# Another order of the mixers' steps: a merge between the two halves of the retention, and a merge ahead of the LRU in the second layer

## The chip, the core and the metric

The kernel is one program on one core of a Trainium2 chip. The metric is the device time of one execution in microseconds (us): the median of three runs before the change is 2495.68 us. The engines of the core run side by side, each through its own fixed list of instructions: PE is TensorE (matrix multiplications), DVE is VectorE, ACT is ScalarE, POOL is GpSimd, SP is SyncE, which here only issues transfers from memory (DMA). An instruction starts when it is at the head of its engine's list and its semaphores are there. So the order in which the lists were written decides who stands behind whom.

## What is computed

Two layers, each a half feed-forward block, a mixer and a second half feed-forward block, on 256 tokens of a sequence ("latent", attending) and 256 tokens of context, 1024 channels. The second layer needs the context only as keys, values and states, so its later work is on 256 columns and that of the first layer on 512. The mixer has four branches (a gated linear recurrence, called LRU, windowed attention GQA, latent attention MLA, and retention), which are merged with gates:

```python
def _gated_merge(branches, gates, w_branch, w_out):
    br = jnp.stack(branches, axis=2)                       # 4 branches of 512 channels
    g = jax.nn.sigmoid(gates.reshape(B, T, N_BRANCH, D_MODEL))
    proj = jnp.einsum('btkw,kwd->btkd', br, w_branch)
    return jnp.einsum('btkd,btkd->btd', g, proj) @ w_out

def _rglru_coeffs(x, w_a, b_a, w_x, b_x, lam):             # LRU, per direction
    r = sigmoid(blockdiag(x, w_a) + b_a)
    i = sigmoid(blockdiag(x, w_x) + b_x)
    log_a = -LRU_C * r * softplus(-lam)
    return exp(log_a), sqrt(1 - exp(2 * log_a)) * (i * x)  # then h = a*h + b over time

# retention, per head, ends with a normalisation of its output:
yn = (y - mean(y)) * rsqrt(var(y) + LN_EPS)                # then * gn_g * silu(dg)
```

The sum over branches k doesn't depend on the order in which they are added, and a branch can be merged as soon as it is there.

## The kernel before

All matrices stand with channels on the 128 partitions and tokens in the columns. A weight tile comes by DMA (`load_w`, L175, three raw buffers), ACT rounds it to fp32r (L178, "hi"), DVE takes the rest (L179, "lo"), and PE runs three fp32r matmuls for each product (`mm3`, L191 to L193). So each weight tile of 128x1024 costs DVE one L179. There are four PSUM buffers "acc", two "s" (`pss`) and two "t" (`pst`).

The mixer runs its steps in the order of a table, `ORDER[l]` (L119 to L122), by `getattr(self, step)(*arg)` (L697), and then `finish` (the output projection and the normalisation). The steps: `gqa_in`, `gqa 0/1`; `mla_in`, `mla 0/1`; `lru_in` (projection and convolution), `lru`, `lru_out` (the gate of the LRU's output); `ret 0/1` (two heads of retention each); `merge k` (branch 0 is the LRU's, 1 GQA, 2 MLA, 3 retention). A scheduler places the instructions of later steps among those of earlier ones where the earlier have to wait, with the earlier step first whenever both are ready. So the table sets priorities, and not strict stages.

Three steps matter for what follows.

`merge k` (L1190) splits its branch (ACT L248, DVE L249, tiles `bh` and `bl`), and then for four pairs of output blocks runs the gates' product (`proj "gt"`), the branch's product, tanh on ACT (L1206), and the gating on DVE (L1212 in the first merge of a mixer, L1215 in others, with an addition on POOL). It is nearly pure PE work: 288 matmuls in the second layer, all on 256 columns. What it needs first from its branch are the tiles of head pair 0, and last those of the last head pair.

`lru` (L744) goes through two halves of four tiles. In each half: gate matmuls L768, tanh, exp, tanh on ACT (L769, L771, L772), DVE L773 to L775; then one sqrt over 128x2048 (L777), which needs another table of functions on ACT than tanh does, so a table load stands before it and one behind it; then matmuls L784, tanh L785, DVE L786 to L788 and two scans L793 and L795 for each tile, POOL L789 and L799. Two buffers `lu` are shared by all of it. In the second layer both halves use the same part of the array `Rall` for L769's result (L758), so the second half's L769 has to wait for the first half's scans and L799.

`ret hp` ends, for each of its two heads, with a chain: scores L1160, weights on DVE L1162, product L1168, two matmuls for mean and square L1175 and L1176, then DVE L1179, L1181, the ten instructions of `rsqrt` (L255 to L265), L1183 and L1185. Only then is the head's branch tile there, which `merge 3` splits.

In the first layer a queue of 24 steps for the modulation vectors (each four DVE instructions L408 on a 512 KB row block `mraw`, which takes one of the three raw buffers) is paced over the mixer's weight loads from the first merge on. The second layer's mixer has none.

Of the kernel before, what the change touches and what calls it, by code (L numbers as in the profile page):

```python
# [54 lines left out]
def host_constants():  # L55
# [40 lines left out]
    for kt in range(2):  # L96
# [20 lines left out]
P = {("g", 0): 20, ("g", 1): 16, "q": 18}  # L117

ORDER = [[("gqa_in",), ("gqa", 0), ("lru_in",), ("gqa", 1), ("mla_in",), ("lru",), ("lru_out",), ("merge", 1),  # L119
          ("mla", 0), ("merge", 0), ("mla", 1), ("ret", 0), ("ret", 1), ("merge", 2), ("merge", 3)],  # L120
         [("gqa_in",), ("gqa", 0), ("gqa", 1), ("mla_in",), ("lru_in",), ("lru",), ("merge", 1), ("mla", 0),
          ("lru_out",), ("mla", 1), ("ret", 0), ("ret", 1), ("merge", 0), ("merge", 2), ("merge", 3)]]  # L122


class Kernel:
# [1186 lines left out]
```

## Time and profile before

| | us |
|---|---|
| median of three runs (2492.79 to 2497.03) | 2495.68 |
| the profiled execution | 2495.55 |
| its span, first to last instruction | 2493.7 |
| PE busy in the span | 2421.7 |
| DVE busy | 1606.7 |
| ACT busy | 1053.7 |
| POOL busy | 389.1 |

The profiled execution is 0.13 us under the median, and 1.85 us of it lie outside the span. The mean granted clock of TensorE is 0.988 of its full 2.4 GHz. In the chain of work that ended last, PE holds 85% of the span, DVE 7%, ACT 3%, DMA 2%.

In rows of instructions the columns are: start (us from the span's start), duration (us), engine, line, operation, out<-in, tile on PE, shape, xcount (neighbours folded into one row), and in brackets the idle time before it and what ended that. An fp32 matmul of 512 columns leaves two records, an fp32r one leaves one. Rows of groups have busy us, mean ns of one, and idle time before with its releasers.

### The profile page before, as it was taken

The page shows a single profiled execution, that of the slowest core. Times are in us where ns is not written, and L with a number is a line of the kernel's source. Part 1 is how long each engine was busy: PE and PEld are TensorE (multiplying, and loading weights), DVE is VectorE, ACT ScalarE, POOL GpSimd, SP SyncE. Part 2 cuts the span into 40 slices and gives each one's busy share as a digit, 9 for nine tenths or more (in the row PEclk, how much of TensorE's full clock was granted, in tenths as well). Part 3 has the DMA queues.
Part 4 walks back from the last instruction along what each step waited for, and adds up shares of the span by engine and source line. Part 5 has one row for each costly group of instructions (what it writes and reads, how often), then busy time and mean ns, then how long its engine had stood idle before and what let it go on. Part 6 is the DMA issues. An engine that isn't in the chain of part 4 may idle for free.

```text
span 2493.7 us, 34785 instructions
## 1 busy us (share of the span) xinstructions
PE 2421.7 (97%) x13320; PEld 2043.8 (82%) x13320; DVE 1606.7 (64%) x2923; ACT 1053.7 (42%) x1694; POOL 389.1 (16%) x411
## 2 busy tenths in 40 slices
PE   7999999999999999999999999999999899999997
PEld 5888888776787778898888898888887678998997
DVE  4963338879857776469833379732388976766554
ACT  4322226665534323352222252322266764455443
POOL 2000024004011112340000220000240112223002
PEclk9999999999999999999999999999999999999999
DMA  8743234122433234437532357833341242465653
GB/s 308 236 136 101 93 108 152 37 89 76 142 88 111 82 97 145 139 120 254 185 93 93 107 174 259 286 100 95 99 145 60 86 128 78 135 194 160 185 177 114
DMA packets 289943, 340.71 MB, mean 137 GB/s; under 512 B 13505, under 2 KB 262625, under 8 KB 289777
## 3 DMA queue, kind: packets, MB, share of 16 engines
q1 hardware_dynamic: 285520, 323.88, 41.3%
q0 software_dynamic: 4256, 14.63, 1.7%
q8 instruction: 104, 1.70, 0.3%
q14 instruction: 63, 0.51, 0.1%
HBM read 334.26 MB, written 4.20 MB: 136 GB/s over the span
## 4 chain that ended last, share of the span: by engine, by line
PE 85%; DVE 7%; ACT 3%; DMA 2%; issue 2%; POOL 1%; SPq 0%; POOLq 0%; DVEq 0%; ACTq 0%
PE ffn01.acc L193 5%; PE ffn01.acc L191 5%; PE ffn01.acc L192 5%; PE ffn00.acc L191 5%; PE ffn00.acc L193 5%; PE ffn00.acc L192 5%; PE ffn10.acc L193 4%; PE ffn10.acc L191 4%; PE ffn10.acc L192 4%; PE ffn11.acc L191 3%; PE ffn11.acc L192 3%; PE ffn11.acc L193 3%; PE merge3.acc L192 1%; PE merge3.acc L191 1%; PE merge3.acc L193 1%
## 5 line engine op out<-in xcount | busy, mean ns | idle before, releaser
L179 DVE TENSOR_TENSOR ffn00.lo<-ffn00.raw,ffn00.hi 128x1024 fp32r<-128x1024 f32 (+1 forms) x71 | 86.5, 1220 | 135.2 <-ACT ffn00.hi L178 135.0
L179 DVE TENSOR_TENSOR ffn01.lo<-ffn01.raw,ffn01.hi 128x1024 fp32r<-128x1024 f32 (+1 forms) x71 | 87.8, 1237 | 128.2 <-ACT ffn01.hi L178 128.1
L179 DVE TENSOR_TENSOR ffn10.lo<-ffn10.raw,ffn10.hi 128x1024 fp32r<-128x1024 f32 (+1 forms) x71 | 87.1, 1226 | 124.9 <-ACT ffn10.hi L178 124.8
L178 ACT CAST ffn10.hi<-ffn10.raw 128x1024 fp32r<-128x1024 f32 (+1 forms) x71 | 72.8, 1025 | 186.5 <-PE ffn10.acc L192 101.9
L178 ACT CAST ffn01.hi<-ffn01.raw 128x1024 fp32r<-128x1024 f32 (+1 forms) x71 | 72.8, 1025 | 178.8 <-PE ffn01.acc L192 144.0
L178 ACT CAST ffn00.hi<-ffn00.raw 128x1024 fp32r<-128x1024 f32 (+1 forms) x71 | 72.5, 1025 | 174.5 <-PE ffn00.acc L192 136.9
L193 PE MATMUL ffn10.acc<-xh,ffn10.lo 128*128 128x512 f32 (+1 forms) x384 | 141.5, 372 | 0.6 <-DVE ffn10.lo L179 0.6
L192 PE MATMUL ffn01.acc<-xl,ffn01.hi 128*128 128x512 f32 (+1 forms) x384 | 142.0, 374 | 0.0
L193 PE MATMUL ffn01.acc<-xh,ffn01.lo 128*128 128x512 f32 (+1 forms) x384 | 141.7, 373 | 0.0
L192 PE MATMUL ffn10.acc<-xl,ffn10.hi 128*128 128x512 f32 (+1 forms) x384 | 141.4, 372 | 0.0
L191 PE MATMUL ffn10.acc<-xh,ffn10.hi 128*128 128x512 f32 (+1 forms) x384 | 140.9, 373 | 0.0
L191 PE MATMUL ffn01.acc<-xh,ffn01.hi 128*128 128x512 f32 (+1 forms) x384 | 140.7, 374 | 0.0
L191 PE MATMUL ffn00.acc<-xh,ffn00.hi 128*128 128x512 f32 x336 | 132.3, 395 | 2.7 <-ACT ffn00.hi L178 2.7
L193 PE MATMUL ffn00.acc<-xh,ffn00.lo 128*128 128x512 f32 x336 | 131.2, 392 | 0.0
L192 PE MATMUL ffn00.acc<-xl,ffn00.hi 128*128 128x512 f32 x336 | 131.1, 391 | 0.0
L179 DVE TENSOR_TENSOR ffn11.lo<-ffn11.raw,ffn11.hi 128x1024 fp32r<-128x1024 f32 x68 | 82.6, 1214 | 75.0 <-ACT ffn11.hi L178 75.0
L191 PE MATMUL ffn11.acc<-xh,ffn11.hi 128*128 128x256 f32 x352 | 99.6, 287 | 4.8 <-ACT xh L248 4.8
L192 PE MATMUL ffn11.acc<-xl,ffn11.hi 128*128 128x256 f32 x352 | 100.1, 286 | 0.0
L193 PE MATMUL ffn11.acc<-xh,ffn11.lo 128*128 128x256 f32 x352 | 99.8, 285 | 0.0
L178 ACT CAST ffn11.hi<-ffn11.raw 128x1024 fp32r<-128x1024 f32 x68 | 69.4, 1021 | 70.2 <-PE ffn11.acc L192 55.6
L193 PEld LDWEIGHTS ffn10.acc<-xh,ffn10.lo 128*128 128x128 f32 x384 | 72.0, 188 | 13.6 <-DVE ffn10.lo L179 1.0
L192 PEld LDWEIGHTS ffn01.acc<-xl,ffn01.hi 128*128 128x128 f32 x384 | 72.6, 190 | 12.7
(679 smaller groups left out, 7783.2 us busy)
## 6 DMA issues: line engine op xcount, KB each, us to landing
ffn10.mraw<-in_w_modT SPq DMA_DIRECT2D x48, 512.0 KB, 5.0
ffn00.raw<-in_ffn_w_in SPq DMA_DIRECT2D x44, 512.0 KB, 4.4
ffn01.raw<-in_ffn_w_in SPq DMA_DIRECT2D x44, 512.0 KB, 3.8
ffn10.raw<-in_ffn_w_in SPq DMA_DIRECT2D x44, 512.0 KB, 4.7
ffn11.raw<-in_ffn_w_in SPq DMA_DIRECT2D x44, 512.0 KB, 3.6
ret.raw<-in_w_in SPq DMA_DIRECT2D x32, 512.0 KB, 3.6
ffn01.mraw<-in_w_modT SPq DMA_DIRECT2D x32, 512.0 KB, 4.5
ffn00.mraw<-in_w_modT SPq DMA_DIRECT2D x24, 512.0 KB, 4.6
```

The lines of the kernel that those rows point to most:

```text
L178: nc.scalar.copy(out=hi[:, :n], in_=raw[:, :n])
L179: nc.vector.tensor_tensor(out=lo[:, :n], in0=raw[:, :n], in1=hi[:, :n].bitcast(F32), op=ALU.subtract)
L191: mm(out, wh, xh, start=start, stop=False)
L192: mm(out, wh, xl, start=False, stop=False)
L193: mm(out, wl, xh, start=False, stop=stop)
```

## The change

Only the table of steps changes.

```diff
-          ("mla", 0), ("merge", 0), ("mla", 1), ("ret", 0), ("ret", 1), ("merge", 2), ("merge", 3)],
-         [("gqa_in",), ("gqa", 0), ("gqa", 1), ("mla_in",), ("lru_in",), ("lru",), ("merge", 1), ("mla", 0),
-          ("lru_out",), ("mla", 1), ("ret", 0), ("ret", 1), ("merge", 0), ("merge", 2), ("merge", 3)]]
+          ("mla", 0), ("merge", 0), ("mla", 1), ("ret", 0), ("merge", 2), ("ret", 1), ("merge", 3)],
+         [("gqa_in",), ("gqa", 0), ("mla_in",), ("gqa", 1), ("lru_in",), ("merge", 1), ("lru",), ("mla", 0),
+          ("lru_out",), ("merge", 0), ("mla", 1), ("ret", 0), ("merge", 2), ("ret", 1), ("merge", 3)]]
```

In the first layer `merge 2` goes between `ret 0` and `ret 1`. In the second layer `mla_in` goes ahead of `gqa 1`, `merge 1` ahead of `lru`, `merge 0` ahead of `mla 1`, and `merge 2` between the two halves of the retention. Every engine has the same number of instructions as before.

On PE, in the second layer, at the LRU's first gate matmuls (L768; `lru_in.g` is the LRU's input, `lru.gw` its gate weights), the list was before:

```order
L192 MATMUL lru_in.acc_15879<-xl_92,lru_in.hi_15912 128x512
L193 MATMUL lru_in.acc_15879<-xh_84,lru_in.lo_15913 128x512
L768 MATMUL lru.pst_15956<-lru_in.g_15868,lru.gw_15950 128x512
L768 MATMUL lru.pst_15966<-lru_in.g_15868,lru.gw_15950 128x512
L191 MATMUL merge1.acc_16136<-xh_77,merge1.hi_16140 128x256
L192 MATMUL merge1.acc_16136<-xl_85,merge1.hi_16140 128x256
L193 MATMUL merge1.acc_16136<-xh_77,merge1.lo_16141 128x256
```

and after the change it is:

```order
L191 MATMUL merge1.acc_16333<-merge1.bh_15953,merge1.hi_16336 128x256
L192 MATMUL merge1.acc_16333<-merge1.bl_15957,merge1.hi_16336 128x256
L193 MATMUL merge1.acc_16333<-merge1.bh_15953,merge1.lo_16337 128x256
L768 MATMUL lru.pst_16372<-lru_in.g_15868,lru.gw_16366 128x512
L768 MATMUL lru.pst_16382<-lru_in.g_15868,lru.gw_16366 128x512
L768 MATMUL lru.pst_16392<-lru_in.g_15873,lru.gw_16366 128x512
L191 MATMUL mla.acc_16542<-mla_in.g_15579,mla.hi_16538 128x512
L192 MATMUL mla.acc_16542<-mla_in.g_15580,mla.hi_16538 128x512
L768 MATMUL lru.pst_16402<-lru_in.g_15873,lru.gw_16366 128x512
```

All 288 matmuls of `merge 1` stood behind the first L768 and now stand ahead of it. Between the first L768 and the first scores of `mla 0` (L882) there were 288 matmuls of `merge 1`, 63 of `mla 0` (12 of them on 512 columns), 23 of `lru_out` and the LRU's 16; now there are 63 of `mla 0`, 45 of `lru_out` and the 16.

On DVE, at the same place, the list was before:

```order
L179 TENSOR_TENSOR merge1.lo_16371<-merge1.raw_16368,merge1.hi_16370 128x1024
L773 TENSOR_SCALAR lru.g_16057<-lru.lu_16058 128x512
L773 TENSOR_SCALAR lru.g_16067<-lru.lu_16068 128x512
L774 SCALAR_TENSOR_TENSOR lru.lu_16058<-R,lru.g_16057 128x512
L179 TENSOR_TENSOR merge1.lo_16407<-merge1.raw_16404,merge1.hi_16406 128x1024
L775 SCALAR_TENSOR_TENSOR lru.g_16057<-lru.lu_16058,lru.g_16057 128x512
L774 SCALAR_TENSOR_TENSOR lru.lu_16068<-R,lru.g_16067 128x512
L179 TENSOR_TENSOR merge1.lo_16441<-merge1.raw_16438,merge1.hi_16440 128x1024
```

and after the change the same part of the LRU (second half, third and fourth tile) reads:

```order
L773 TENSOR_SCALAR lru.g_16473<-lru.lu_16474 128x512
L774 SCALAR_TENSOR_TENSOR lru.lu_16474<-R,lru.g_16473 128x512
L775 SCALAR_TENSOR_TENSOR lru.g_16473<-lru.lu_16474,lru.g_16473 128x512
L773 TENSOR_SCALAR lru.g_16483<-lru.lu_16484 128x512
L1046 COPY mla.g_16549<-mla_in.g_15529 32x512
L774 SCALAR_TENSOR_TENSOR lru.lu_16484<-R,lru.g_16483 128x512
L786 SCALAR_TENSOR_TENSOR lru.lu_16494<-lru.lu_16494,lru_in.g_15940 128x512
L775 SCALAR_TENSOR_TENSOR lru.g_16483<-lru.lu_16484,lru.g_16483 128x512
```

The subtractions and gatings of `merge 1` have left the LRU's part of the list; the copies of `mla 0` that its scores need (L1046, L1058, L1080, L1081) stand among or behind the LRU's last instructions.

On DVE, in the first layer, at the first head of `ret 0` (the list of weights L1147 and the first products L1162), the list was before:

```order
L179 TENSOR_TENSOR ret.lo_7230<-ret.raw_7227,ret.hi_7229 128x1024
L1136 SCALAR_TENSOR_TENSOR ret.g_6995<-ret.tmp_6993,ret.acc_6931 128x512
L179 TENSOR_TENSOR ret.lo_7270<-ret.raw_7267,ret.hi_7269 128x1024
L1136 SCALAR_TENSOR_TENSOR ret.g_6999<-ret.tmp_6997,ret.acc_6932 128x512
L1147 SCALAR_TENSOR_TENSOR ret.g_7001<-mla.g_6629,ffn00.lg_583,ret.tmp_7003 128x512
L1162 SCALAR_TENSOR_TENSOR ret.SW_7012<-ret.pss_7013,ret.g_7001 128x256
```

and after the change it is:

```order
L1136 SCALAR_TENSOR_TENSOR ret.g_6995<-ret.tmp_6993,ret.acc_6931 128x512
L408 SCALAR_TENSOR_TENSOR merge2.ht_7339,merge1.part_5008<-merge2.mraw_7337,merge2.sb_7183 128x512
L408 SCALAR_TENSOR_TENSOR merge2.ht_7341,merge1.part_5008<-merge2.mraw_7337,merge2.sb_7183 128x512
L179 TENSOR_TENSOR merge2.lo_7280<-merge2.raw_7277,merge2.hi_7279 128x1024
L1136 SCALAR_TENSOR_TENSOR ret.g_6999<-ret.tmp_6997,ret.acc_6932 128x512
L1147 SCALAR_TENSOR_TENSOR ret.g_7001<-mla.g_6629,ffn00.lg_583,ret.tmp_7003 128x512
L408 SCALAR_TENSOR_TENSOR merge2.ht_7343,merge1.part_5008<-merge2.mraw_7337,merge2.sb_7183 128x512
L408 SCALAR_TENSOR_TENSOR merge2.ht_7345,merge1.part_5008<-merge2.mraw_7337,merge2.sb_7183 128x512
L1162 SCALAR_TENSOR_TENSOR ret.SW_7012<-ret.pss_7013,ret.g_7001 128x256
```

Steps of the modulation queue that came with `merge 2` behind `ret 1` now stand ahead of the first L1162 of `ret 0`; their first L408 waits for a DMA of `mraw`.

## Rows read from the trace of the kernel before

**Rows 1.** The page's head and its first section, the whole span.
```profile
span 2493.7 us, 34785 instructions
PE 2421.7 (97%) x13320; PEld 2043.8 (82%) x13320; DVE 1606.7 (64%) x2923; ACT 1053.7 (42%) x1694; POOL 389.1 (16%) x411
```

**Rows 2.** Stretches: length, busy us by engine (records), granted clock, DMA share, GB/s.
```profile
816.00:862.00 46.00, 44.25 (x186) 34.00 (x186) 32.21 (x61) 15.47 (x24) 6.61 (x6) 1.00 0.24 70
878.00:930.00 52.00, 47.53 (x189) 36.54 (x188) 38.68 (x72) 15.30 (x24) 7.80 (x5) 0.93 0.28 84
894.30:901.00 6.70, 6.69 (x19) 5.44 (x20) 4.29 (x13) 0.37 (x1) 0.00 (x0) 0.60 0.25 77
1865.00:1930.00 65.00, 64.88 (x337) 47.19 (x336) 54.91 (x148) 40.35 (x91) 1.85 (x3) 1.00 0.20 62
1930.00:2011.00 81.00, 69.75 (x407) 56.49 (x407) 74.56 (x116) 54.45 (x75) 13.92 (x15) 0.92 0.32 96
...
2184.00:2253.00 69.00, 69.00 (x577) 69.00 (x576) 42.78 (x54) 34.64 (x52) 17.20 (x22) 1.00 0.64 195
```

**Rows 3.** PE's instructions in order of time, 1929 to 2017, second layer's LRU.
```profile
1930.04 1.88 PE L768 MATMUL lru.pst<-lru_in.g,lru.gw 128*128 128x512 f32 x4
...
1958.18 5.39 PE L768 MATMUL lru.pst<-lru_in.g,lru.gw 128*128 128x512 f32 x8 [2.79 <-ACT lru.lu L785]
...
2011.01 1.96 PE L882 MATMUL mla.pss<-mla.g,mla.q 96*128 96x512 f32 x4 [0.26 <-DVE mla.q L1080]
```

**Rows 4.** PE's groups of instructions, 1930 to 2011.
```profile
L768 PE MATMUL lru.pst<-lru_in.g,lru.gw 128*128 128x512 f32 x16 | 9.5, 718 | 2.8 <-ACT lru.lu L785 2.8
...
L193 PE MATMUL mla.acc<-mla_in.g,mla.lo 128*128 128x512 f32 x4 | 2.2, 600 | 1.3 <-DVE mla.lo L179 1.3
```

**Rows 5.** DVE's groups of instructions, 1930 to 2011.
```profile
L179 DVE TENSOR_TENSOR merge1.lo<-merge1.raw,merge1.hi 128x1024 fp32r<-128x1024 f32 x11 | 14.3, 1312 | 0.0
L788 DVE TENSOR_TENSOR lru.lu<-lru.lu,R 128x512 f32<-128x512 f32 x8 | 7.9, 1003 | 0.3 <-ACT R L777 0.3
...
L1212 DVE SCALAR_TENSOR_TENSOR R<-merge1.sa,merge1.acc 128x256 f32<-128x256 f32 x8 | 3.3, 412 | 1.5 <-PE merge1.acc L193 0.9 <-issue 0.5
L773 DVE TENSOR_SCALAR lru.g<-lru.lu 128x512 f32<-128x512 f32 x8 | 3.2, 416 | 0.0
```

**Rows 6.** ACT's groups of instructions, 1930 to 2011.
```profile
L771 ACT ACTIVATE lru.lu<-R,ffn00.c 128x512 f32<-128x512 f32 x8 | 6.3, 810 | 4.0 <-DVE R L795 2.8 <-DVE lru.g L775 1.2
...
L785 ACT ACTIVATE lru.lu<-lru.pst,ffn00.hb 128x512 f32<-128x512 f32 x8 | 5.3, 687 | 4.1 <-DVE R L795 4.1
L769 ACT ACTIVATE R<-lru.pst,ffn00.hb 128x512 f32<-128x512 f32 x8 | 5.2, 679 | 2.3 <-PE lru.pst L768 2.3
```

**Rows 7.** ACT in order of time, 1929 to 1960, around the first half's sqrt.
```profile
1945.74 1.28 ACT L777 ACT_TABLE_LOAD   x1
1947.04 1.92 ACT L777 ACTIVATE R<-R 128x2048 f32<-128x2048 f32 x1
1948.97 1.28 ACT L785 ACT_TABLE_LOAD   x1
```

**Rows 8.** PE in order of time, last head of the second layer's `ret 1`.
```profile
2158.41 0.61 PE L1176 MATMUL ret.pss<-ret.tmp,ffn10.onesh 128*128 128x256 f32 x2
```

**Rows 9.** DVE in order of time, the same head's chain, first and last instruction.
```profile
2160.05 0.41 DVE L1179 TENSOR_TENSOR ret.q<-ret.q,ret.pss 128x256 f32<-128x256 f32 x1
...
2167.87 0.64 DVE L1185 TENSOR_TENSOR ret.q<-ret.q,ret.q 128x256 f32<-128x256 f32 x1
```

**Rows 10.** PE in order of time, 886 to 905, first layer's `ret 1`, first head.
```profile
894.31 2.08 PE L1160 MATMUL ret.pss<-ret.g,ret.g 128*128 128x256 f32 x4 [3.87 <-DVE ret.SW L1162]
```

**Rows 11.** DVE in order of time, 880 to 940: that head's wait, then the second head's chain.
```profile
886.52 0.69 DVE L408 SCALAR_TENSOR_TENSOR merge2.ht<-merge2.mraw,ret.sb 128x512 bf16<-128x512 f32 x1 [3.87 <-DMA merge2.mraw<-in_w_modT]
...
922.46 0.69 DVE L1179 TENSOR_TENSOR ret.g<-ret.g,ret.pss 128x512 f32<-128x512 f32 x1 [2.48 <-ACT ret.tmp L1178]
...
935.49 0.69 DVE L1185 TENSOR_TENSOR ret.g<-ret.g,ret.g 128x512 f32<-128x512 f32 x1
```

## Prediction

> **What bounds the kernel now.** The page's first section comes first: PE is busy for 2421.7 of 2493.7 us [rows 1], so the time is PE's work plus the stretches in which PE waits. The change keeps every instruction, so it can only move those waits. Next I read the busy times by stretch. The merges of the second layer run without a gap: 577 matmuls of 256 columns in 69.00 us, 0.1196 us each [rows 2]. The waits that the change can reach are in three places. One is the LRU of the second layer (1930 to 2011): PE busy 69.75 of 81.00 us at a granted clock of 0.92, DVE busy 74.56 [rows 2]. The others are the retention's ends in the first layer: `ret 0` at 816 to 862, 1.75 us idle, and `ret 1` at 878 to 930, 4.47 us idle at a clock of 0.93 [rows 2]. The stretch of `gqa 1` and `mla_in` ahead of the LRU has PE at 64.88 of 65.00 us [rows 2], so there is nothing to gain there; exchanging these two is costed at nothing, and its cover is `lru_in` and `merge 1`, which are ready there.
>
> **The LRU of the second layer, before.** From the first L768 at 1930.04 to the first score of `mla 0` at 2011.01 [rows 3] there are 81.0 us. PE's work in them by count: the window has 407 records, of which 32 are the LRU's 16 fp32 matmuls (16 records of L768, and as many of L784), 12 are on 512 columns (three groups of four) [rows 4], and 363 on 256 (one stray one of 512 among them). At 0.1196 us these 363 are 43.4 us; the 12 at twice that are 2.9; four records of L768 took 1.88 us [rows 3], 0.9 us for a matmul without the last one's run-out, so 14.4 for 16. That makes 60.7 us of work and a **loss of 20.3 us**. DVE set the pace: it was busy 92% of the stretch, and in that, beside the LRU, it did 11 subtractions of `merge 1` (14.3 us) and its 8 gatings L1212 (3.3 us) [rows 5].
>
> **The same, after.** All 288 matmuls of `merge 1` now stand ahead of the first L768, where `gqa 1` and `lru_in` cover them. Behind it, up to the first score, PE's list holds 96 matmuls of 256 columns (11.5 us), the 12 (2.9) and the LRU's 16 (14.4): 28.8 us. How long the stretch becomes is DVE's and ACT's matter, since the scores need L1080 and L1081, which stand behind the LRU on DVE. From above: 81.0 less the 17.6 us of `merge 1` on DVE is 63.4. From below: the LRU's own work on DVE is eight groups of eight instructions, from L788 with 7.9 us to L773 with 3.2 [rows 5], 44.0 in all, and some 5 us of copies, rope and one or two subtractions stand in it, 49. To that come waits which `merge 1` filled on DVE before: each half's sqrt takes 1.28 + 1.92 + 1.28 us with its two table loads [rows 7], 4.5, under which DVE has one L775 (0.7) left, so 7.6 for both halves; the first load, L769 and L771 before DVE can begin (1.28 + 0.68 + 0.81, by [rows 6, 7]), 2.8; and the second half's L769, which waits for scans and POOL of the first, with ACT's waits for L795 of 2.8 and 4.1 us [rows 6] as the nearest rows, 3. That is 62.4. I take **62 us**, since both ways come out there. The loss becomes 62 - 28.8 = 33.2, **12.9 us more**. Bounds: 57 us (bare work and the sqrts alone), +7.9; 67 us (63.4, and eight of the LRU's matmuls on the chain at the 1.35 us of four in 5.39 [rows 3]), +17.9.
>
> The row shows what a table load does to ACT: it starts at 1945.74, takes 1.28 us, and the sqrt starts at 1947.04, with no further gap [rows 7]. The Trainium skill says otherwise ("ScalarE: Activation LUTs", section "What ACT_TABLE_LOAD costs"): a switch of tables costs the 1.28 us and a drain of about 1.38 us. By that the four loads inside the LRU would add an estimated 5.5 us to the chain; by the trace they add none, and I go by the trace.
>
> **Leaving the LRU.** After 3.87 us of idle PE [rows 10] the granted clock was 0.60 for the next 6.70 us [rows 2], half speed for most of it: 2.7 us lost. `mla 0` now starts after far more idle time. I add **2.5 us** (0 to 4).
>
> **merge 3 at the end of the second layer.** Before, `merge 0` and `merge 2` stood between `ret 1` and `merge 3`; now `merge 3` follows at once, and needs the last head's tile. From L1176 at 2158.41 [rows 8] to L1179 at 2160.05, then to L1185 at 2167.87 [rows 9]: 7.8 us, of which 0.7 was two L1215 that are gone from there, so 7.1; with 1.0 ahead, 0.6 for L1185 and 0.4 for the split, 9.1 us behind L1176. PE's list has 39 matmuls there, 4.7 us. PE waits 4.4; I take **4 us** (2 to 6).
>
> **merge 3 in the first layer.** The same, with 512 columns: L1179 at 922.46 to L1185 at 935.49 [rows 11] is 13.0 us, and with 0.9 ahead, 0.7 for L1185 and 0.7 for the split, 15.3. PE's list has 56 matmuls at 0.24, 13.4. **2 us** (0 to 4).
>
> **ret 0 in the first layer.** Its DVE list now has the modulation steps and weights of `merge 2` ahead of the first L1162, as `ret 1` had before. There an L408 waited 3.87 us for its `mraw` [rows 11], the head's weights came late, and PE idled 3.87 us [rows 10] and then ran at a clock of 0.60 [rows 2]. `ret 1` lost 4.47 + 2.7 = 7.2 us, `ret 0` 1.75; copying the pattern costs 5.4. It may be that the transfer is in time here, which costs nothing; I take **4** (0 to 5.4), nearer to the row. `ret 1` keeps its own pattern, as `merge 3` brings the modulation steps that `merge 2` brought, so nothing is won back. `merge 0` and `merge 2` of the second layer, as near-pure PE work, cost nothing where they now stand.
>
> **The sum**, against the profiled execution's 2495.55 us: 12.9 + 2.5 + 4 + 2 + 4 = 25.4, 2521 us; that execution lies 0.13 under the median, which changes nothing.
>
> **Rivals.**
> - *The LRU at its bare pace, and the tails filled (faster).* Free of `merge 1`, DVE goes through the LRU in 49 us, where the waits for sqrt are covered by the other tiles; then the loss is 49 - 28.8 = 20.2, as before. And `merge 2` as filler takes away the idle time and the half clock of the first layer's two tails, 7.2 + 1.75. Time 2487. It decides at 49 us from the first L768 to the first L882. For it: DVE was busy 92% there. Against it: the sqrt covers all four tiles of a half, and the second half's L769 has to wait for the first half's scans. Chance 0.06.
> - *The LRU only a little longer, tails as before.* 53 to 55 us, +4 to +6, the wait of `merge 3` in the second layer at 2 to 4, nothing at `ret 0`. Time 2503. For it: the 63.4 still holds the end of `lru_in` on DVE, which now runs under `merge 1`. Chance 0.15.
> - *The clock makes the LRU itself longer.* PE idles more than half of the stretch. Matmuls at the half clock took 1.35 us instead of 0.9 [rows 3], and 67 us for the LRU, the full 5.4 at `ret 0`, 6 at `merge 3`, 4 on leaving and 2 in the first layer make +35: 2531. Chance 0.16. The Trainium skill ("TensorE: Matmul & The Clock Gate", section "HAM oscillation — how this bites in real kernels") says that waits between bursts of matmuls throw the clock back to half again and again; by it an estimated 57.6 us of PE work at half speed would still fit under the 62, so that only the LRU's own matmuls would count, and the rows here (0.92 with 20 us lost) show it only in part.
> - *The scheduler undoes the order.* 2495.6. The lists show all of `merge 1` ahead of L768, so this is out but for small effects that cancel: 0.05.
>
> **How the numbers follow.** The forecast has 0.58, the others as given. The range leaves out the faster case and the unchanged one: from 2503 (the second rival) to 2536 (the sum of all upper bounds, 17.9 + 4 + 6 + 4 + 5.4, is 2533; some room for transfers). A difference of 0.2%, 5 us, is about what can be told from no change. Faster by that: 0.07; within it: 0.06; slower: 0.87.
>
> **What would show it.** In the changed kernel's trace the distance from the first L768 to the first L882 of the second layer should be 57 to 67 us with PE busy under 60% and a granted clock well under 0.92; L191 of `merge 3` on the last head's `bh` should wait for ACT L248 by 2 to 6 us in the second layer; the first L1160 of `ret 0` in the first layer should wait for DVE L1162 some 4 us with an L408 ahead of it waiting for DMA. The forecast is wrong if the LRU ends within 50 us, or if `merge 1` ahead of the LRU itself waits for the tiles of `gqa 1`, which I costed at nothing.

## The result, and the profile after

The changed kernel takes 2512.99 us (median of four runs, 2511.75 to 2515.33); the kernel before, in four runs, 2494.80. The ratio is 1.0080, with an interval of 1.0068 to 1.0092: **18.2 us slower**. The forecast was 2521 us, 26 above the 2494.80, with a range of 2503 to 2536. Direction and range held; the sum was some 7 us too high.

The head of the page of the changed kernel, with its first section, beside [rows 1]:

```profile
span 2509.6 us, 34780 instructions
## 1 busy us (share of the span) xinstructions
PE 2423.1 (97%) x13320; PEld 2042.2 (81%) x13320; DVE 1608.4 (64%) x2923; ACT 1053.8 (42%) x1694; POOL 387.7 (15%) x411
```

PE, DVE, ACT and POOL have as many instructions as before, and PE is busy for 1.4 us more; the span has grown by 15.9. So the time went into PE's waits and into slower matmuls, and the stretches show where. Busy times of the changed kernel by stretch (columns as in [rows 2]: length, busy time and records of PE, PEld, DVE, ACT, POOL, granted clock, DMA share, GB/s): `ret 0` and `ret 1` of the first layer; of the second layer `gqa 1` and its neighbours, the LRU up to the first scores, the 7 us behind it, and `merge 3` on the last head's tile:

```profile
816.00:862.00 46.00, 43.84 (x184) 33.56 (x183) 32.68 (x57) 14.76 (x23) 7.84 (x5) 1.00 0.27 81
930.00:985.00 55.00, 53.09 (x265) 42.88 (x265) 41.14 (x86) 16.57 (x26) 7.83 (x5) 1.00 0.35 106
1865.00:1930.00 65.00, 63.04 (x345) 47.68 (x346) 54.70 (x142) 40.56 (x89) 0.73 (x1) 1.00 0.16 45
1961.00:2023.00 62.00, 41.21 (x145) 24.96 (x143) 52.63 (x83) 40.20 (x52) 12.82 (x15) 0.75 0.13 37
2023.00:2030.00 7.00, 6.66 (x32) 4.42 (x33) 6.72 (x17) 2.73 (x6) 0.00 (x0) 1.00 0.71 181
2244.00:2253.00 9.00, 5.98 (x28) 5.98 (x29) 6.79 (x13) 3.41 (x7) 3.60 (x4) 0.62 0.39 113
```

The fourth row is the one to look at. Before, the LRU had 81 us with PE at 69.75 and a clock of 0.92 [rows 2]. Now it has 62 us with PE at 41.2 and a clock of 0.75: `merge 1` no longer fills it. PE's timeline in the second layer of the changed kernel, at `merge 1`, the LRU, the first scores, and `merge 3`:

```profile
1925.64 0.38 PE L193 MATMUL merge1.acc<-xh,merge1.lo 128*128 128x256 f32 x1 [1.96 <-DVE merge1.lo L179]
...
1943.98 0.39 PE L191 MATMUL merge1.acc<-xh,merge1.hi 128*128 128x256 f32 x1 [1.52 <-ACT merge1.sa L1206]
...
1961.37 2.94 PE L768 MATMUL lru.pst<-lru_in.g,lru.gw 128*128 128x512 f32 x6
...
1976.73 2.08 PE L784 MATMUL lru.pst<-lru_in.g,lru.gw 128*128 128x512 f32 x2 [4.10 <-ACT lru.lu L785]
1984.39 5.49 PE L768 MATMUL lru.pst<-lru_in.g,lru.gw 128*128 128x512 f32 x6 [4.07 <-ACT lru.lu L785]
...
2002.75 1.12 PE L784 MATMUL lru.pst<-lru_in.g,lru.gw 128*128 128x512 f32 x2 [2.93 <-ACT lru.lu L785]
...
2011.40 0.58 PE L191 MATMUL mla.acc<-mla_in.q,mla.hi 128*128 128x256 f32 x1 [4.85 <-DVE mla.g L1058]
...
2023.18 1.96 PE L882 MATMUL mla.pss<-mla.g,mla.q 96*128 96x512 f32 x4 [0.20 <-DVE mla.q L1080]
...
2247.02 1.01 PE L191 MATMUL merge3.acc<-merge3.bh,merge3.hi 128*128 128x256 f32 x3 [3.73 <-ACT merge3.bh L248]
```

To put all of it on one scale I count for every stretch the matmuls in it, at the duration that their shape has at full clock (0.1196 us for 256 columns, as in the prediction), and call length less that work the **loss**: it holds idle time and half-clock time together. The stretches left out lose as much as before, within 0.3 us.

| stretch | loss before, us | loss after, us |
|---|---|---|
| first layer, mixer up to `ret` | 26.7 | 26.1 |
| first layer, `ret` to `finish` | 16.2 | 12.3 |
| end of the MLP between, to the second layer's `gqa_in` | 3.6 | 0.7 |
| second layer, `gqa_in` to the first L768 | 12.7 | 16.7 (5.2 of it in `merge 1`) |
| first L768 to first L882 | 21.2 | 33.9 |
| `mla 0` to `ret` | 2.6 | 2.0 |
| `ret` and what follows, to `finish` | 6.2 | 13.5 |

The differences add up to 16.0 us, and the span grew by 15.9. Two of the rows swing between runs of kernels that are alike in that place. The end of the MLP had 0.7 to 3.8 in the profiles of the experiments below, one apart that has fewer scratch tiles. The first layer's `ret` to `finish` had 12.6 to 14.4 in five further profiles with its old order, and 11.7 to 12.3 in seven of the eight with the new one (14.4 in the other). The losses that count are the three of the second layer: +4.0, +12.7 and +7.3.

### The profile page after: what moved, and what is told of

It is laid out like the page before. It is cut to its first block, busy times and chain, and to the rows that moved or that the text cites. A ratio compares the mean times of both kernels' runs of the same rounds, so it can differ in the third digit from the quotient of the medians.

```text
span 2509.6 us, 34780 instructions
## 1 busy us (share of the span) xinstructions
PE 2423.1 (97%) x13320; PEld 2042.2 (81%) x13320; DVE 1608.4 (64%) x2923; ACT 1053.8 (42%) x1694; POOL 387.7 (15%) x411
## 4 chain that ended last, share of the span: by engine, by line
PE 86%; DVE 6%; ACT 3%; DMA 3%; issue 1%; POOL 1%; SPq 0%; POOLq 0%; DVEq 0%; ACTq 0%
PE ffn01.acc L191 5%; PE ffn01.acc L192 5%; PE ffn01.acc L193 5%; PE ffn10.acc L193 5%; PE ffn10.acc L192 5%; PE ffn10.acc L191 5%; PE ffn00.acc L191 5%; PE ffn00.acc L193 5%; PE ffn00.acc L192 5%; PE ffn11.acc L191 3%; PE ffn11.acc L192 3%; PE ffn11.acc L193 3%; PE mla.pss L882 1%; PE ret.acc L191 1%; PE ret.acc L192 1%
## 5 line engine op out<-in xcount | busy, mean ns | idle before, releaser
L179 DVE TENSOR_TENSOR ffn00.lo<-ffn00.raw,ffn00.hi 128x1024 fp32r<-128x1024 f32 (+1 forms) x71 | 86.5, 1220 | 135.1 <-ACT ffn00.hi L178 135.0
L179 DVE TENSOR_TENSOR ffn01.lo<-ffn01.raw,ffn01.hi 128x1024 fp32r<-128x1024 f32 (+1 forms) x71 | 87.8, 1236 | 127.2 <-ACT ffn01.hi L178 127.1
L179 DVE TENSOR_TENSOR ffn10.lo<-ffn10.raw,ffn10.hi 128x1024 fp32r<-128x1024 f32 (+1 forms) x71 | 87.1, 1227 | 125.3 <-ACT ffn10.hi L178 125.1
L179 DVE TENSOR_TENSOR ffn11.lo<-ffn11.raw,ffn11.hi 128x1024 fp32r<-128x1024 f32 x68 | 82.7, 1216 | 74.6 <-ACT ffn11.hi L178 74.6
L193 PEld LDWEIGHTS ffn10.acc<-xh,ffn10.lo 128*128 128x128 f32 x384 | 72.0, 188 | 12.8 <-DVE ffn10.lo L179 0.4
L193 PEld LDWEIGHTS ffn01.acc<-xh,ffn01.lo 128*128 128x128 f32 x384 | 72.0, 188 | 12.5
```

The source lines that it names most:

```text
L179: nc.vector.tensor_tensor(out=lo[:, :n], in0=raw[:, :n], in1=hi[:, :n].bitcast(F32), op=ALU.subtract)
L193: mm(out, wl, xh, start=False, stop=stop)
```

## The experiments

Where nothing else is said, the diff is against the kernel before, and losses are counted as above.

### Each layer by itself

`l0_only` has the changed row of the first layer alone:

```diff
-          ("mla", 0), ("merge", 0), ("mla", 1), ("ret", 0), ("ret", 1), ("merge", 2), ("merge", 3)],
+          ("mla", 0), ("merge", 0), ("mla", 1), ("ret", 0), ("merge", 2), ("ret", 1), ("merge", 3)],
```

> Only the first layer's table is changed (merge 2 between ret 0 and ret 1); the second layer is as before. Theory A, from the trace after the change: the first layer gains some 4 us, since ret 1's half-clock stretch (4.0 us idle and 2.7 us of clock) shrinks to a 1.1 us wait: 2491 us. Theory B, the prediction's terms (ret 0 takes over ret 1's pattern, +4, and merge 3 waits, +2): 2501 us.

Measured: 2489.91 against 2490.68 us, ratio 0.9996 (0.9987 to 1.0005). **No change**; the 6 us that the prediction gave the first layer are not there.

`l1_only` has the changed row of the second layer alone:

```diff
-         [("gqa_in",), ("gqa", 0), ("gqa", 1), ("mla_in",), ("lru_in",), ("lru",), ("merge", 1), ("mla", 0),
-          ("lru_out",), ("mla", 1), ("ret", 0), ("ret", 1), ("merge", 0), ("merge", 2), ("merge", 3)]]
+         [("gqa_in",), ("gqa", 0), ("mla_in",), ("gqa", 1), ("lru_in",), ("merge", 1), ("lru",), ("mla", 0),
+          ("lru_out",), ("merge", 0), ("mla", 1), ("ret", 0), ("merge", 2), ("ret", 1), ("merge", 3)]]
```

> Only the second layer's table is changed; the first layer is as before. Theory A: all of the loss is here, +13 at the LRU, +4 in merge 1 ahead of it and +7 at merge 3: 2495 + 22 to 24 = 2517 to 2519 us. Theory B, the prediction's terms for this layer (12.9 + 2.5 + 4): 2514 us, and the rest of the measured 18 us from the first layer.

Measured: 2512.33 against 2490.68 us, ratio 1.0087 (1.0074 to 1.0101): 21.6 us more. The LRU's stretch is 61.2 us long with a loss of 33.3, `ret` and `merge 3` lose 12.2. **All of the change's loss is in the second layer.**

### The parts of the second layer

`merge1_first` moves only `merge 1` ahead of `lru`:

```diff
-         [("gqa_in",), ("gqa", 0), ("gqa", 1), ("mla_in",), ("lru_in",), ("lru",), ("merge", 1), ("mla", 0),
+         [("gqa_in",), ("gqa", 0), ("gqa", 1), ("mla_in",), ("lru_in",), ("merge", 1), ("lru",), ("mla", 0),
```

> The kernel before with only merge 1 ahead of lru in the second layer's table. Theory A: what drives merge 1 ahead of the LRU on PE is that the LRU's gate weights share the two PT buffers with gqa 1's attention, and so come late only when gqa 1 is late too; with gqa 1 in its old place, 260 of the 288 matmuls of merge 1 stay beside the LRU, and the time is 2495 to 2499 us. Theory B: the table's order alone costs the 13 us: 2508 us or more.

Measured: 2501.61 against 2490.68 us, ratio 1.0044 (1.0030 to 1.0058), 10.9 us more. PE's list is not that of the changed kernel: 28 matmuls of `merge 1`, three L768, the other 260 (two of them among the three), and then the LRU's remaining 13 nearly alone. PE's timeline of `merge1_first` at the LRU:

```profile
1928.76 1.02 PE L768 MATMUL lru.pst<-lru_in.g,lru.gw 128*128 128x512 f32 x2
...
1979.68 4.53 PE L768 MATMUL lru.pst<-lru_in.g,lru.gw 128*128 128x512 f32 x6 [5.44 <-ACT lru.lu L785]
...
1998.14 2.08 PE L784 MATMUL lru.pst<-lru_in.g,lru.gw 128*128 128x512 f32 x2 [2.92 <-ACT lru.lu L785]
```

and its busy times from the first L768 to the first scores:

```profile
1928.80:2017.90 89.10, 70.47 (x403) 54.41 (x401) 73.71 (x110) 54.00 (x72) 12.87 (x15) 0.83 0.31 95
```

`merge 1` lies inside this stretch, and yet the loss is 30.0 us against 21.2 before, at a clock of 0.83 against 0.92. It is not enough that the filler stands in the stretch. With `merge 1` first in rank, PE runs it through wherever it is ready, and when the LRU's waits come, it is used up.

`swap_in` only exchanges `mla_in` and `gqa 1`:

```diff
-         [("gqa_in",), ("gqa", 0), ("gqa", 1), ("mla_in",), ("lru_in",), ("lru",), ("merge", 1), ("mla", 0),
+         [("gqa_in",), ("gqa", 0), ("mla_in",), ("gqa", 1), ("lru_in",), ("lru",), ("merge", 1), ("mla", 0),
```

> The kernel before with only mla_in ahead of gqa 1 in the second layer's table. Theory A: the gate weights come late, so 83 of merge 1's matmuls go ahead of the first L768 and 205 stay beside the LRU; a third of the LRU's 13 us, +3 to +6: 2498 to 2501 us. Theory B (the prediction costed this exchange at nothing): 2495 us.

Measured: 2502.96 against 2490.68 us, ratio 1.0047 (1.0034 to 1.0059). **12.3 us more, for an exchange that the prediction costed at nothing.** PE's timeline of `swap_in` at the LRU's start:

```profile
1943.82 5.46 PE L768 MATMUL lru.pst<-lru_in.g,lru.gw 128*128 128x512 f32 x6 [4.07 <-DMA lru.gw<-in_lru_g]
```

and its busy times in two stretches, the 24 us ahead of the first L768, and from there to the first scores:

```profile
1919.60:1943.80 24.20, 18.18 (x134) 15.71 (x133) 15.89 (x36) 12.25 (x24) 1.13 (x2) 0.91 0.46 145
1943.80:2018.40 74.60, 58.45 (x319) 46.60 (x319) 61.94 (x97) 46.25 (x64) 12.79 (x15) 0.87 0.24 74
```

The gate weights `gw` of the LRU (L752) take their buffers from the pair "PT", which the two heads of `gqa` use for their probabilities (L877). The view of that tile gives its DMA's first and last issue, in `swap_in`:

```profile
L754 POOL DMA_DIRECT2D lru.gw<-in_lru_g x2: 540/564/587, 1936.9 to 1937.5; - x2
```

and in the kernel before:

```profile
L754 POOL DMA_DIRECT2D lru.gw<-in_lru_g x2: 540/564/587, 1909.1 to 1909.7; - x2
```

With `gqa 1` behind `mla_in` it frees the pair 28 us later, PE waits 4.07 us for the transfer, and until then 83 matmuls of `merge 1` have run ahead of the first L768. The loss from `gqa_in` to the first scores is 45.6 us against 33.8.

`tail_only` has the changed second line of the second layer's row alone (`merge 0` ahead of `mla 1`, `merge 2` between the halves, `merge 3` last behind `ret 1`):

```diff
-          ("lru_out",), ("mla", 1), ("ret", 0), ("ret", 1), ("merge", 0), ("merge", 2), ("merge", 3)]]
+          ("lru_out",), ("merge", 0), ("mla", 1), ("ret", 0), ("merge", 2), ("ret", 1), ("merge", 3)]]
```

> The kernel before with only the end of the second layer's table changed: merge 0 ahead of mla 1, merge 2 between ret 0 and ret 1, merge 3 last. The LRU stays as before. Theory A, from the trace after the change: merge 3 waits 3.7 us for the last head's tile and then runs some 6 us at half clock, 6 to 8 us over before. Theory B: the merges between hide other waits of the mla and ret heads, and the end costs 0 to 3 us in all.

Measured: 2497.60 against 2491.92 us, ratio 1.0023 (1.0013 to 1.0032), 5.7 us more. PE's timeline of `tail_only` at `merge 3`:

```profile
2232.46 0.63 PE L191 MATMUL merge3.acc<-merge3.bh,merge3.hi 128*128 128x256 f32 x3 [3.72 <-ACT merge3.bh L248]
```

and its busy times in the 5.6 us behind that wait:

```profile
2232.40:2238.00 5.60, 5.50 (x30) 5.25 (x31) 4.29 (x8) 3.04 (x7) 3.62 (x4) 0.70 0.20 62
```

3.72 us of waiting, and then 30 matmuls in 5.5 us, where full clock needs 3.6: together 5.6 us, the time that the run is longer by.

`no_end_wait` is the changed kernel with the end of the second layer as before:

```diff
-          ("lru_out",), ("merge", 0), ("mla", 1), ("ret", 0), ("merge", 2), ("ret", 1), ("merge", 3)]]
+          ("lru_out",), ("mla", 1), ("ret", 0), ("ret", 1), ("merge", 0), ("merge", 2), ("merge", 3)]]
```

> The changed kernel, but with the second layer's end as before (ret 0, ret 1, merge 0, merge 2, merge 3). Theory A: only the LRU's part of the loss is left, 15 to 17 us over before less about 2 us of the first layer: 13 to 15 us over before. Theory B (the prediction's size, 4 us for merge 3): 4 us less than the changed kernel, 18 us over before.

Measured: 2505.81 against 2491.92 us, ratio 1.0053 (1.0036 to 1.0070), 13.9 us more than before. The LRU's stretch is as in the changed kernel (61.4 us, loss 33.5), and the end loses 6.3 us again. 13.9 and the 5.7 of `tail_only` make 19.6, the change's 18.2 to 21.6. But `merge1_first` and `swap_in` make 23.2 where both together cost 13.9: **these two don't add**, since each of them takes the same work of `merge 1` away from the LRU's waits.

### Can the LRU's waits be filled otherwise?

Both kernels here have the first layer as changed and the second as before but for one step.

`fill_mlain` puts `mla_in` behind `merge 1`, as a further filler:

```diff
-         [("gqa_in",), ("gqa", 0), ("gqa", 1), ("mla_in",), ("lru_in",), ("lru",), ("merge", 1), ("mla", 0),
+         [("gqa_in",), ("gqa", 0), ("gqa", 1), ("lru_in",), ("lru",), ("merge", 1), ("mla_in",), ("mla", 0),
```

> First layer as changed; in the second layer mla_in goes behind merge 1 (gqa_in, gqa 0, gqa 1, lru_in, lru, merge 1, mla_in, mla 0, lru_out, then as before). Theory A: the LRU's stretch lacks PE work, and 19 us of projection behind merge 1 fill the waits ahead of mla 0's scores: 5 to 9 us under before. Theory B: mla_in is needed where it was, beside gqa 1's heads, and the LRU's gate weights come late: 5 us or more over before.

Measured: 2502.47 against 2491.92 us, ratio 1.0035 (1.0022 to 1.0048), 10.5 us more. The stretch now holds more work (it is 105.3 us long) and loses 28.2 us, 7 more than before: `mla_in` has a chain of its own at its end, where PE waits 3.19 us for ACT L966 and 1.94 for L248, right ahead of `mla 0`.

`fill_lruout` puts `lru_out` ahead of `mla 0`:

```diff
-         [("gqa_in",), ("gqa", 0), ("gqa", 1), ("mla_in",), ("lru_in",), ("lru",), ("merge", 1), ("mla", 0),
-          ("lru_out",), ("mla", 1), ("ret", 0), ("ret", 1), ("merge", 0), ("merge", 2), ("merge", 3)]]
+         [("gqa_in",), ("gqa", 0), ("gqa", 1), ("mla_in",), ("lru_in",), ("lru",), ("merge", 1), ("lru_out",),
+          ("mla", 0), ("mla", 1), ("ret", 0), ("ret", 1), ("merge", 0), ("merge", 2), ("merge", 3)]]
```

> First layer as changed; in the second layer lru_out goes ahead of mla 0 (lru, merge 1, lru_out, mla 0, mla 1, then as before). Theory A: 8 us more of PE work ahead of mla 0's scores shorten the waits at the LRU's end by 3 to 6 us, and mla 0's heads are filled by mla 1's and ret 0's projections: 3 to 6 us under before. Theory B: the mla heads then lack filler, 0 to 5 us over before.

Measured: 2491.18 against 2491.92 us, ratio 0.9994 (0.9984 to 1.0003). No change.

### The exchange without its price

`swap_in_gw` is `swap_in` with a buffer of its own for the gate weights of the first half; to make room, the scratch tiles `h` go from five to three:

```diff
-        return self.p_tmp.tile([128, L], F32, tag=f"h{s}", bufs=5, name=self.name("ht"))
+        return self.p_tmp.tile([128, L], F32, tag=f"h{s}", bufs=3, name=self.name("ht"))
-            w = self.p_g.tile([128, 4, L], F32, tag="PT", bufs=2, name=self.name("gw"))
+            w = self.p_g.tile([128, 4, L], F32, tag="PT" if self.both or cp else "gw", bufs=2 if self.both or cp else 1, name=self.name("gw"))
```

> swap_in (mla_in ahead of gqa 1, else as before), with one edit: the first half's LRU gate weights of the second layer have a buffer of their own, and not one of the two PT buffers that gqa 1's attention holds; to make room the rope's scratch tiles have three buffers instead of five. Theory A: swap_in lost its 12 us because the gate weights came late (PE waited 4.07 us for that DMA, and merge 1 was spent before the LRU): now the LRU starts early again and most comes back, 0 to 4 us over before. Theory B: it is the plan of the lists, with merge 1's matmuls ahead of the LRU, and the wait for the weights is only seen there: still 7 to 13 us over before.

Measured: 2496.86 against 2492.68 us, ratio 1.0019 (1.0010 to 1.0028), 4.2 us more, where `swap_in` cost 12.3. The loss from `gqa_in` to the first scores is 33.0 us, against 45.6 in `swap_in` and 33.8 before: the price of the exchange is gone there. The order of PE's list changed with the buffer too (56 matmuls of `merge 1` ahead of the first L768, 83 in `swap_in`), so how much of the price was the wait itself and how much the order isn't shown. What remains lies in front of `gqa_in`, where this run loses 11.1 us and others 0.7 to 3.8; it has fewer scratch tiles. So the next kernel takes a buffer that costs no scratch.

`ss_swap` has the first layer as changed, the exchange, the rest of the second layer as before, and the first half's gate weights in the tile "ss", which is there for the layer norm and idle at that time:

```diff
-            w = self.p_g.tile([128, 4, L], F32, tag="PT", bufs=2, name=self.name("gw"))
-            w = w.rearrange("p a c -> p (a c)").rearrange("p (k d i c) -> p k d i c", k=2, d=2, i=2)
+            if self.both or cp:
+                w = self.p_g.tile([128, 4, L], F32, tag="PT", bufs=2, name=self.name("gw"))
+                w = w.rearrange("p a c -> p (a c)")
+            else:
+                w = self.p_tmp.tile([128, 1024], F32, tag="ss", bufs=1, name=self.name("gw"))
+            w = w.rearrange("p (k d i c) -> p k d i c", k=2, d=2, i=2)
```

> As swap_in_gw, but the first half's gate weights lie in the normalisation's 4 KB scratch tile, which nobody uses during the second layer's mixer, so that no other buffer is made smaller; the first layer as changed. Theory A: the 4 us that swap_in_gw was still over before came from the scratch tiles cut from five to three (its trace lost some 9 us behind the first layer's second feed-forward), and not from the LRU: 0 to 4 us under before. Theory B: the exchange of mla_in and gqa 1 itself costs: 3 to 6 us over before.

Measured: 2487.36 against 2492.47 us, ratio 0.9977 (0.9968 to 0.9986): **5.1 us faster than the kernel before**, and the best of all. The view of the tile `gw` in `ss_swap`:

```profile
L758 POOL DMA_DIRECT2D lru.gw<-in_lru_g x2: 587/587/587, 1825.7 to 1936.7; - x2
```

and its busy times from the first L768 to the first scores:

```profile
1936.09:2004.81 68.72, 59.37 (x353) 48.54 (x352) 62.57 (x102) 47.88 (x67) 14.60 (x16) 0.93 0.33 102
```

The first half's weights are fetched 110 us before they are needed. 56 matmuls of `merge 1` run ahead of the first L768, the other 232 stand spread among the LRU's 16, and the stretch loses 15.5 us. From `gqa_in` on it is 31.4, against 33.8 before. Once the transfer is out of its way, the exchange costs nothing. Whether the gain comes from it, or from the earlier weights alone, isn't shown: the other buffer was not tried without the exchange. Of the 5.1 us these losses show 2.4; the first layer's new order, which is in this kernel too, may hold most of the rest (some 2 us by the profiles, but 0.8 in `l0_only`, which can't be told from nothing).

### DVE's share in the LRU

`pool_lo` has the first layer as changed, the second as before, and gives POOL every third of the twelve L179 of `merge 1` in the second layer:

```diff
-        nc.vector.tensor_tensor(out=lo[:, :n], in0=raw[:, :n], in1=hi[:, :n].bitcast(F32), op=ALU.subtract)
+        eng = nc.vector
+        if self.lab == "merge1" and self.l == 1:
+            self.nlo = getattr(self, "nlo", 0) + 1
+            eng = nc.gpsimd if self.nlo % 3 == 0 else nc.vector
+        eng.tensor_tensor(out=lo[:, :n], in0=raw[:, :n], in1=hi[:, :n].bitcast(F32), op=ALU.subtract)
```

> First layer as changed, second layer's table as before, and four of merge 1's twelve weight subtractions in the second layer (those of the branch weights) run on POOL instead of DVE. Theory A: DVE sets the pace of the LRU's stretch (92% busy), so taking 4 x 1.3 us off it shortens the stretch by 4 to 6 us: 4 to 6 us under before. Theory B: the chain through ACT, sqrt and the two lu buffers sets it, or POOL's slower subtraction (some 4 us for 1024 columns, from 1.05 us for 256 in L799) holds PE up: no gain, or 0 to 5 us over before.

Measured: 2488.52 against 2492.68 us, ratio 0.9984 (0.9975 to 0.9993), 4.2 us faster. Busy times of `pool_lo` from 1925 to 2005, which holds the LRU:

```profile
1925.00:2005.00 80.00, 68.45 (x409) 54.96 (x408) 78.29 (x119) 54.13 (x75) 20.47 (x18) 0.96 0.31 95
```

and DVE's group of L788 (here L792) in that stretch:

```profile
L792 DVE TENSOR_TENSOR lru.lu<-lru.lu,R 128x512 f32<-128x512 f32 x8 | 11.3, 1428 | 0.0
```

DVE lost four subtractions and is busier than before, 98% against 92%: its own instructions became longer (last section). The loss of the LRU's stretch falls by only 1.5 us, from the 20.4 of `l0_only` to 18.9. That is less than half of the 4.2 us; the new order of the first layer is in this kernel too, and the rest has no place.

`ss_swap_pool` joins the edits of `ss_swap` and `pool_lo`.

> ss_swap with four of merge 1's twelve weight subtractions on POOL, as in pool_lo. Theory A: the two effects add, 4 to 7 us under before. Theory B: DVE is at its limit in the LRU's stretch either way and the two give the same microseconds: 2 to 4 us under before.

Measured: 2493.23 against 2492.47 us, ratio 1.0001 (0.9992 to 1.0010). The two gains don't add; they cancel. The LRU's stretch loses 19.9 us here, 15.5 in `ss_swap`.

## Why the prediction was right, point by point

**The LRU (forecast +12.9, measured +12.7).** The term that carries the forecast came out at its size: 62 us from the first L768 to the first scores was 61.8, 28.8 us of PE work was 27.9, a loss of 33.2 was 33.9 (21.2 before by the same count, forecast 20.3). That it came out so near is luck in part, as two misses in the working from below cancelled. DVE's groups of the changed kernel from the first L768 to the first scores, and its timeline behind the LRU:

```profile
L788 DVE TENSOR_TENSOR lru.lu<-lru.lu,R 128x512 f32<-128x512 f32 x8 | 7.0, 888 | 1.8 <-ACT R L777 1.8
L179 DVE TENSOR_TENSOR lru_out.lo<-lru_out.raw,lru_out.hi 128x1024 fp32r<-128x1024 f32 x4 | 5.2, 1307 | 0.5 <-ACT lru_out.hi L178 0.5
...
2017.98 0.01 DVE L819 LOAD_MASK_SELECT mla.ht<-mla.q  x1 [1.18 <-ACT mla.q L1071]
```

DVE waited 1.8 us for the two sqrts, where the working had 7.6: under each of them it had L786 and L787 of the first tile to do beside L775, and it didn't wait for the second table load. The LRU's own groups take 43.7 us, as forecast (44.0); but the other work that stands in the stretch on DVE takes some 12 us by the same groups, 5.2 of it four subtractions of `lru_out`, where the working had 5. DVE's idle time in all is some 9 us instead of 13.4. PE was busy for 66% of the stretch and not for under 60%, since a matmul at half clock counts as busy for longer.

The mechanism is in ACT's timeline of the changed kernel:

```profile
1971.48 1.28 ACT L777 ACT_TABLE_LOAD   x1
...
1977.08 0.69 ACT L785 ACTIVATE lru.lu<-lru.pst,ffn00.hb 128x512 f32<-128x512 f32 x1 [0.40 <-DVE R L795]
...
1983.65 0.69 ACT L785 ACTIVATE lru.lu<-lru.pst,ffn00.hb 128x512 f32<-128x512 f32 x1 [5.88 <-DVE R L795]
1984.75 0.69 ACT L769 ACTIVATE R<-lru.pst,ffn00.hb 128x512 f32<-128x512 f32 x1 [0.41 <-POOL lru_in.g L799]
```

ACT's L785 waits 5.88 us for the scan that frees a buffer, the second half's L769 for POOL L799 of the first half, and PE for ACT: 4.10, 4.07 and 2.93 us in the rows above. The steps hold each other, and nothing is left to fill with. The rival of the bare LRU (49 us, nothing lost) is out by 12.8 us, that of 53 to 55 us by 7 or more. The rival of the clock was right that half clock comes (0.75 in the stretch), and right only in small part that it makes the stretch longer: of the 61.8 us some 1.2 are the clock's (next paragraph), not 5. Its price was misread too: three of the LRU's matmuls at a granted clock of 0.50 took 5.49 us (at 1984.39 above), 1.83 each and not 1.35. The Trainium skill's drain behind a table load ("ScalarE: Activation LUTs", section "What ACT_TABLE_LOAD costs") isn't in the changed kernel either: the load at 1971.48 takes 1.28 us, and the sqrt starts at 1972.77.

**Leaving the LRU (forecast +2.5, measured 0 behind the scores).** In the 7 us behind the first scores the granted clock is 1.00. The half clock came, but ahead of the scores. Busy times of the changed kernel behind the wait of 4.85 us that ends at 2011.40:

```profile
2011.40:2017.30 5.90, 5.90 (x27) 5.90 (x28) 5.22 (x9) 0.80 (x1) 1.56 (x2) 0.50 0.02 3
```

27 matmuls of `mla 0` take 5.9 us at 0.50, where full clock needs 3.2. They and then `lru_out`'s stand ahead of the scores, and the clock is back before these. So the price lies inside the stretch, where the loss of 33.9 holds it already, and DVE's work covers part of it: DVE waits only 1.18 us for L1071, which follows these matmuls. As an estimate from that row, some 1.2 us of the 61.8 are the clock's. The step that failed is the place: the term was added behind the stretch, to matmuls that no longer pay it.

**merge 3 of the second layer (forecast +4, measured 5.7 by `tail_only`, 7.3 by the losses).** The wait is 3.73 us, the 4.4 of the working nearly. The term is too small since it left out the half clock behind the wait, which the prediction itself had priced for other places: in the changed kernel the 28 matmuls from 2247.0 to 2253.0 take 6.0 us instead of 3.3, at a granted clock of 0.50.

**The first layer (forecast +2 and +4, measured 0).** `l0_only` shows no change. One of the two waits came, but too small to count; the other didn't come. DVE's timeline of the changed kernel at L408, first in `ret 0`, then in `ret 1`, and PE's at the first L1160 of each:

```profile
825.74 0.69 DVE L408 SCALAR_TENSOR_TENSOR merge2.ht<-merge2.mraw,merge2.sb 128x512 bf16<-128x512 f32 x1 [2.60 <-DMA merge2.mraw<-in_w_modT]
...
948.20 0.69 DVE L408 SCALAR_TENSOR_TENSOR merge3.ht<-merge3.mraw,merge2.sb 128x512 bf16<-128x512 f32 x1 [5.43 <-DMA merge3.mraw<-in_w_modT]
...
831.50 1.13 PE L1160 MATMUL ret.pss<-ret.g,ret.g 128*128 128x256 f32 x4 [1.55 <-DVE ret.SW L1162]
...
956.99 1.13 PE L1160 MATMUL ret.pss<-ret.g,ret.g 128*128 128x256 f32 x4 [0.90 <-DVE ret.SW L1162]
```

In `ret 0` PE waits 1.55 us for L1162 (0.90 before), where the forecast had some 4, and no half clock follows. In `ret 1` DVE's wait is longer than the 3.87 us of [rows 11], but PE now has `merge 2` to do: its own wait falls from 3.87 us [rows 10] to 0.90, and the stretch runs at 1.00 instead of 0.93. PE shows no wait of `merge 3` for the last head's tile: DVE needs 11.4 us from L1179 (983.19) to L1185 (994.60), not 13.0 [rows 11], and PE's matmuls cover it. The step that failed is "`ret 1` keeps its own pattern, so nothing is won back": it gives back more than `ret 0` pays. Whether a small gain stays can't be told by the times: 0.8 us, from 3.2 less to 1.2 more; the profiles, with 11.7 to 12.3 us in seven of eight against 12.6 or more, speak for some 2 us.

**The exchange and merge 1 ahead (forecast 0, measured +4.0 in place).** Here the prediction named a way in which it could fail, and it came in another form: `merge 1` ahead of the LRU waits itself, but not for the tiles of `gqa 1`; it waits 1.96 us for its weights from L179 and 1.52 for L1206. Worse, "costed at nothing" was read from PE alone (64.88 of 65.00 us busy). The exchange by itself costs 12.3 us, through a transfer whose buffer `gqa 1` holds; inside the change most of this doesn't show, since the LRU has lost its filler anyway. Its issue moved there too, from 1909.1 to this row of the changed kernel's POOL timeline:

```profile
1931.88 1.13 POOL L754 DMA_DIRECT2D lru.gw<-in_lru_g  x2 [43.67 <-issue]
```

**The sum.** Of the forecast's 25.4, the first layer's 6 weren't there, and the 2.5 for leaving the LRU lie in the LRU's own 12.7; 4.0 ahead of the first L768 and up to 3.3 more at `merge 3` weren't in it. The three losses of the second layer make 12.7 + 4.0 + 7.3 = 24.0, which the interval of `l1_only` holds (18 to 25 us); the change's 18.2 lies at its lower end, with the two swinging rows of the table 6.8 us lower than in the execution of before. So the sum came out near because the misses went both ways.

**What stays open.** Why the losses differ by 1 to 4 us between runs at places that the kernels share. At one of them it is the clock: in the first layer's `ret` to `finish`, with the old order, PE waits 2.8 to 3.9 us at `ret 1`, and the half clock then costs 2.7 us in the kernel before, up to 1.7 in four others and nothing in `l1_only`; why it differs isn't shown. And why `merge1_first` mixes three L768 into `merge 1`, while the changed kernel's list has all 288 matmuls ahead of the first. Late gate weights are not the reason: with a buffer of their own for them, the changed kernel's list still has all 288 ahead.

## What to carry to other kernels

Where a scheduler places work by rank, work that fills the waits of a chain must stand behind the chain: put ahead of it, it runs where PE was busy anyway, and the chain runs bare. Before a step is called free to move, look at which buffers it holds and who else draws from them: a 512 KB transfer of another step, 28 us late, made a harmless exchange cost 12 us, and with an idle buffer the same exchange cost nothing. Price a wait on PE with the half clock that can follow it, at the place where it follows: here, behind waits of 3.7 to 4.9 us, 27 and 28 matmuls lost 2.7 us each time, once on the path and once for the most part hidden by DVE.

## What the runs showed of the hardware

DVE instructions that meet a subtraction on POOL get several times longer. POOL's timeline of `pool_lo`, two of its subtractions:

```profile
1942.44 2.38 POOL L183 TENSOR_TENSOR merge1.lo<-merge1.raw,merge1.hi 128x1024 fp32r<-128x1024 f32 x1 [18.01 <-DVE lru.g L777]
...
1961.05 2.51 POOL L183 TENSOR_TENSOR merge1.lo<-merge1.raw,merge1.hi 128x1024 fp32r<-128x1024 f32 x1
```

and DVE's of the same kernel, three of L774 (here L778) and one of L788 (here L792):

```profile
1936.75 0.68 DVE L778 SCALAR_TENSOR_TENSOR lru.lu<-R,lru.g 128x512 f32<-128x512 f32 x1
1939.61 0.69 DVE L778 SCALAR_TENSOR_TENSOR lru.lu<-R,lru.g 128x512 f32<-128x512 f32 x1
1942.62 2.75 DVE L778 SCALAR_TENSOR_TENSOR lru.lu<-R,lru.g 128x512 f32<-128x512 f32 x1
...
1961.28 2.83 DVE L792 TENSOR_TENSOR lru.lu<-lru.lu,R 128x512 f32<-128x512 f32 x1
```

0.68 us become 2.75 and 2.83, and each ends 0.55 us after POOL's instruction does (1944.82 and 1945.37; 1963.56 and 1964.11): DVE stood still until POOL was done. The Trainium skill says so ("SBUF — State Buffer", section "SBUF: two separate sides"): DVE instructions with two inputs in SBUF share a pair of ports with POOL, and whoever begins first holds it for its whole instruction; these rows agree. All four subtractions that went to POOL met such an instruction, which took 2.3 to 2.8 us: in the LRU each cost DVE some 2.1 us, more than the 1.3 that it saved. So DVE won nothing by it; why the LRU's stretch still loses 1.5 us less isn't shown. It is also the likely reason, which wasn't tried by itself, why L788 already took 1.0 us in the kernel before [rows 5]: with POOL's L789 beside it, it took 0.8 to 1.1 us there, and 0.69 where POOL was idle.
